# Low weights of the first gate block meet both token tiles at once, and the second tile's norm, quarters and norm row come in another order

## The chip, the cores and the metric

The kernel runs on one core of a Trainium2 chip. A core has five engines with a queue each: TensorE (PE in the profile, with its weight loads as PEld), VectorE (DVE), ScalarE (ACT), GpSimd (POOL) and SyncE (SP, which here only issues DMAs). The metric is the device time of one execution in microseconds; the median of the runs counts.

## The reference

One decoder layer on 256 tokens of width 2048, in float32. The part around the change is the end of the mixing sub-layer and the beginning of the channel mixer:

```python
mix = jnp.concatenate([o_a, o_b], axis=-1) @ w_out[l]
x = x + rmsnorm(mix, post_mix_g[l])
h = rmsnorm(x, pre_ffn_g[l])
u = causal_dwconv(h @ w_up[l], conv_w[l], conv_b[l])
gate, val = jnp.split(u, 2, axis=-1)
y = (jax.nn.gelu(gate, approximate=True) * val) @ w_down[l]
x = x + rmsnorm(y, post_ffn_g[l])
```

`rmsnorm(x, g)` is `x * rsqrt(mean(x*x) + 1e-6) * g` for each token. `w_up` has 2 x 5632 columns; the first 5632 are the gate, the others the value.

## The kernel before

**Products in two parts.** Every float32 operand of a matmul is split into a high part (rounded to the type that TensorE takes) and a low part (what is left), and a product is high x high + high x low + low x high. For weights, ScalarE casts the high part out of a loaded buffer `raw` and VectorE subtracts it to get the low part (`w_split`, lines 112 and 115; `w_high`, lines 95 and 98, where the low part is a function of its own that is called later). There are five `raw` buffers and five slots each for high and low parts, so a load waits for an earlier unit's low part, and a cast waits until TensorE is done with an earlier unit. For activations, `hT` holds for each of 16 chunks of 128 channels (kt) 512 columns: 256 of high parts (128 for each of two token tiles) and 256 of low parts. One matmul of high weights against all 512 columns gives two of the three products; one of low weights against the 256 high columns gives the third. A bank of 512 columns collects them; `conv` (line 908) adds its two halves.

**Around the change.** The output projection's last two column quarters (n = 2 and 3 of four quarters of 512 columns) are computed tile by tile (`out_cols`, line 800). For each, VectorE scales and adds the bank into `mix`, ScalarE squares and sums it into `msq`, and GpSimd multiplies it by the norm's gain `gbc` (`evac_b`, line 747). When a tile has all its sums, `mix_rstd` (line 764) takes VectorE's sum and scaling and GpSimd's power of -1/2, and `residual` (line 769) adds `mix` times that to the tokens `x_sb`, quarter by quarter on VectorE. `turn` (line 773) then transposes a quarter of a tile on TensorE (four transposes into one bank), and its two returned functions write the high parts (ScalarE, line 783) and the low parts (VectorE, line 788) of four chunks of `hT`.

**The first gate block.** The first 256 gate columns have their weights loaded ahead, as four units of four chunks (`gate_unit`, line 828; `lows[0]` to `lows[2]` are the low weights of units 1 to 3). So that TensorE can begin before the second tile is there, `first_gate` (line 924) works tile by tile: `one(t, u)` runs unit u for tile t, eight high products of 256 columns (line 947; that tile's high and low columns) and eight low products (line 943). Units 0 and 1 run their low products for each tile alone, 128 columns; units 2 and 3 run them once, for both tiles, 256 columns, with tile 1. The order on TensorE is: tile 0 units 0 to 2, the sixteen transposes of tile 1, tile 0 unit 3, tile 1 units 0 to 3.

**The norm row.** The second norm's factor for each token is not applied to `hT`; it is made into a row (`rowf`) and multiplied in behind the projection. `x_squares` (line 795) sums each token's squares on ScalarE, four instructions for a tile. `ffn_tables` (line 870) turns them into a factor (VectorE, GpSimd) and a diagonal matrix, and returns `rows`, which transposes the convolution's weights (line 879) and spreads the two diagonals over all partitions by matmul (`row_of`, line 209). `rows` runs in the first value projection (`proj_T4`, line 272) at its first tick, behind the sixteen highs and sixteen lows of units 0 and 1.

**What sets the order.** TensorE's instructions keep the program's order throughout. From line 810 to the end of `first_gate` (line 1074) ScalarE, VectorE and GpSimd keep the order of the text too; instructions from outside this stretch, such as the casts and subtractions of the next projections' weights, may be put between them by a planner that works with estimated times. Elsewhere the planner sets the order of those three engines. `hold.__exit__` (line 859) frees memory that the convolution's table `cst` and the down projection's buffer `extra` take over, so the DMA issues into `cst`, which stand in ScalarE's queue (lines 865 and 866), wait for the last instruction that reads `gbc`.

Of the kernel before, what the change touches and what calls it, by code (L numbers as in the profile page):

```python
# [8 lines left out]
F32 = mybir.dt.float32  # L9
# [8 lines left out]
P = 128  # L18
S = 256
D = 2048  # L20
# [11 lines left out]
def hybrid_layer(ctx: ExitStack, tc: tile.TileContext, x, pre_mix_g, w_in, b_forget, sinks,  # L32
# [27 lines left out]
    def later(n, f):  # L60
        todo.setdefault(now[0] + n, []).append(f)
# [207 lines left out]
            high(*steps[-1])  # L269
            tick()  # L270

    def proj_T4(w, c0, banks):


        parts = {}

        def get(*us):
            for u in us:
                parts[u] = w_split(w_load(w_rows(w, u * 4, 4, c0, 256), 4, 256), still=True)

        def high(kt):
            u, a = divmod(kt, 4)
            for m, b in enumerate(banks):
                pe.matmul(b, parts[u][0][:, a, m * P:(m + 1) * P], hT[:, kt, :],  # L284
                          start=(kt == 0), stop=(kt == KT - 1))

        def low(kt):
            u, a = divmod(kt, 4)
            for m, b in enumerate(banks):
                pe.matmul(b[:, 256:512], parts[u][1][:, a, m * P:(m + 1) * P],  # L290
                          hT[:, kt, 0:256], start=False, stop=False)

        get(0, 1)
        for kt in range(8):
            high(kt)
        for kt in range(8):
            low(kt)
        tick()
        get(2, 3)
        for kt in range(8, 16):  # L300
            low(kt)
        for kt in range(8, 16):
            high(kt)
# [11 lines left out]
    with tc.tile_pool(name="mixp", bufs=1) as mp:  # L315
# [448 lines left out]
        def mix_rstd(t):  # L764
            st = small.tile([P, 1], F32, tag="st", name="st_m")
            dve.tensor_reduce(st, msq[t][:, 0:4 + t], axis=AX.X, op=ALU.add)
            rmix.append(rstd_of(st, D, f"rmix{t}"))

        def residual(t, n):
            xs = x_sb[:, t, n * 512:(n + 1) * 512]  # L770
            dve.scalar_tensor_tensor(xs, mix[t][n], rmix[t], xs, op0=ALU.mult, op1=ALU.add)

        def turn(t, n):

            tb = bank("att")
            for j in range(4):
                c = n * 512 + j * P
                pe.transpose(tb[:, j * P:(j + 1) * P], x_sb[:, t, c:c + P], ident)
            kts = [(n * 4 + j, tb[:, j * P:(j + 1) * P]) for j in range(4)]

            def high():
                for kt, b in kts:
                    act.activation(hT[:, kt, t * P:(t + 1) * P], b, AF.Copy,
                                   scale=gcol[:, 16 + kt:17 + kt])

            def low():
                for kt, b in kts:
                    dve.scalar_tensor_tensor(hT[:, kt, 256 + t * P:256 + (t + 1) * P], b,
                                             gcol[:, 16 + kt:17 + kt],
                                             hT[:, kt, t * P:(t + 1) * P].bitcast(F32),  # L790
                                             op0=ALU.mult, op1=ALU.subtract)

            return high, low
# [51 lines left out]
        lows[0]()  # L845
        for _, low in turns:
            low()
        evac_b(1, 2, out_cols(2, 1, slice(0, 256)), 0)
        lows[1]()
        turns = [turn(0, 2), turn(0, 3)]  # L850
        for high, _ in turns:
            high()
        turns[0][1]()
        evac_b(1, 2, out_cols(2, 1, slice(256, 512)), 1)
        turns[1][1]()
        mix_rstd(1)
        for n in range(4):
            residual(1, n)
        hold.__exit__(None, None, None)

# [1 line left out]
    with tc.tile_pool(name="ffn", bufs=1) as fp:  # L862
# [61 lines left out]
        def first_gate():  # L924

            banks = [bank(), bank()]

            def one(t, u):
                ts = slice(t * P, t * P + P)

                both = u >= 2
                ls = slice(0, 256) if both else ts

                def v(x):
                    return x.rearrange("p (h t c) -> p h t c", h=2, t=2)[:, :, t, :]

                for low in (False, True)[:1 if both and t == 0 else 2]:
                    for kt in range(u * 4, u * 4 + 4):
                        hi, lo = gate[kt]
                        for m, b in enumerate(banks):  # L940
                            ms = slice(m * P, (m + 1) * P)
                            if low:
                                pe.matmul(b[:, 256 + ls.start:256 + ls.stop], lo[:, ms],
                                          hT[:, kt, ls], start=False,
                                          stop=(t == 1 and kt == KT - 1))
                            else:
                                pe.matmul(v(b), hi[:, ms], v(hT[:, kt, :]),
                                          start=(t == 0 and kt == 0), stop=False)

            one(0, 0)  # L950
            one(0, 1)
            one(0, 2)
            for high, low in [turn(1, u) for u in range(4)]:
                high()
                low()
            one(0, 3)
            lows[2]()
            x_squares(0)
            x_squares(1)
            for t in range(2):  # L960
                act.dma_start(x_dram[t * P:(t + 1) * P, :], x_sb[:, t, :])
            rows = ffn_tables()
            for u in range(4):
                one(1, u)
            later(1, rows)
            return banks

        def token_sums(into, y0, y1):

# [94 lines left out]
        for half in range(2):  # L1064
# [4 lines left out]
            for g in range(FHALF // 2):  # L1069
                c0 = (half * (FHALF // 2) + g) * 256  # L1070
                alt = g % 2
                if half == 0 and g == 0:
                    bg = first_gate()
                    order.__exit__(None, None, None)
                    bv = [bank(), bank()]
                    proj_T4(w_up, DFF + c0, bv)
                else:
                    bg = [bank("att"), bank("att")] if alt else [bank(), bank()]
                    proj_T4(w_up, c0, bg)
                gates, ys = [], []  # L1080
# [181 lines left out]
```

## Time and profile before

| | us |
|---|---|
| median of 3 runs | 1063.35 |
| lowest and highest | 1061.34, 1063.37 |
| the profiled execution's own time | 1063.75 |
| its span, first to last instruction | 1062.0 |
| busy in it: TensorE, VectorE, ScalarE, GpSimd | 1047.4, 849.2, 638.4, 227.5 |

The profile is of one execution; all its times count from the start of its span. A row of the chain of waits has a start, a length and a group of instructions; a row of the timeline has a start, a length, engine, line, operation, the tile written and those read, a count, and in brackets how long the engine had been idle and what ended that. Rows of one line's instructions give shortest, median and longest duration in ns. Instructions of an engine overlap a little, so that a group's length over its count is the rate, not the time of one.

### The profile page before, as it was taken

What the parts mean: (1) busy time and instruction counts of PE and PEld (TensorE: products, weight loads), DVE (VectorE), ACT (ScalarE), POOL (GpSimd) and SP (SyncE); (2) the same over time, 40 slices, a digit from 0 to 9 for tenths busy, and PEclk for the clock granted to TensorE, in tenths of its full rate; (3) what the DMA queues carried; (4) which work ended last, traced back from release to release, by engine and by line L of the source; (5) the groups of instructions that cost most, each with busy time, mean ns of one, the idle gap of its engine ahead of it and who ended that gap; (6) DMA issues with size and microseconds to landing.
All of it is one profiled execution on the core that took longest, in us unless ns stands there. A gap on an engine that the chain in (4) does not pass through costs nothing.

```text
span 1062.0 us, 16259 instructions
## 1 busy us (share of the span) xinstructions
PE 1047.4 (99%) x5874; PEld 911.7 (86%) x5874; DVE 849.2 (80%) x1393; ACT 638.4 (60%) x1096; POOL 227.5 (21%) x256
## 2 busy tenths in 40 slices
PE   9999999999999999999999999999999999999995
PEld 7889988888889888888888888888888888888884
DVE  5988888997568887788767989668778787789987
ACT  6767667767547765556555555446556565656551
POOL 3253334441122121212112000012121221200004
PEclk9999999999999999999999999999999999999998
DMA  8645566554863866656665556656566665656562
GB/s 286 211 120 168 164 209 204 177 162 153 301 222 110 293 218 197 192 179 191 194 198 179 198 199 213 220 181 198 168 209 188 192 197 184 196 175 201 196 249 108
DMA packets 154284, 207.08 MB, mean 195 GB/s; under 512 B 6844, under 2 KB 131036, under 8 KB 153180
## 3 DMA queue, kind: packets, MB, share of 16 engines
q1 hardware_dynamic: 153200, 203.37, 59.7%
q10 hardware_dynamic: 1004, 2.68, 0.6%
q8 instruction: 46, 0.75, 0.3%
q14 instruction: 34, 0.28, 0.1%
HBM read 201.68 MB, written 4.21 MB: 194 GB/s over the span
## 4 chain that ended last, share of the span: by engine, by line
PE 75%; DVE 15%; issue 3%; ACT 3%; DMA 2%; POOL 1%; DVEq 0%; SPq 0%; POOLq 0%; ACTq 0%
PE bank_acc L284 15%; PE bank_att L284 14%; PE bank_acc L309 10%; PE bank_acc L290 8%; PE bank_att L290 7%; PE bank_acc L253 7%; DVE wlo L313 6%; PE bank_att L982 4%; PE bank_acc L258 3%; DVE wlo L115 1%; DMA extra<-in_w_down_dram 1%; PE bank_att L475 1%; DVE tb L1026 1%; PE bank_att L511 1%; DVE tb L1023 1%
## 5 line engine op out<-in xcount | busy, mean ns | idle before, releaser
L115 DVE TENSOR_TENSOR wlo<-raw,whi 128x1024 fp32r<-128x1024 f32 (+3 forms) x271 | 329.9, 1228 | 123.6 <-ACT whi L112 116.2
L112 ACT CAST whi<-raw 128x1024 fp32r<-128x1024 f32 (+3 forms) x270 | 273.1, 1029 | 128.2 <-issue 86.0
L914 POOL TENSOR_TENSOR room<-room,rowf 128x256 f32<-128x256 f32 x88 | 100.3, 1160 | 393.9 <-DVE room L913 392.0
L284 PE MATMUL bank_acc<-hT,whi 128*128 128x512 f32 x736 | 173.3, 390 | 0.0
L284 PEld LDWEIGHTS bank_acc<-hT,whi 128*128 128x128 f32 x736 | 136.4, 188 | 27.4
L982 PE MATMUL bank_att<-whi,G 128*128 128x512 f32 x488 | 156.1, 389 | 0.0
L284 PE MATMUL bank_att<-hT,whi 128*128 128x512 f32 x640 | 150.6, 390 | 0.0
L284 PEld LDWEIGHTS bank_att<-hT,whi 128*128 128x128 f32 x640 | 118.7, 188 | 23.9
L982 PEld LDWEIGHTS bank_att<-whi,G 128*128 128x128 f32 x488 | 91.6, 188 | 18.8
L982 PE MATMUL bank_att<-wlo,G 128*128 128x512 f32 x244 | 95.2, 390 | 0.1
L290 PEld LDWEIGHTS bank_acc<-hT,wlo 128*128 128x128 f32 x736 | 89.3, 188 | 2.0
L290 PE MATMUL bank_acc<-hT,wlo 128*128 128x256 f32 x736 | 89.8, 279 | 0.0
L916 ACT ACTIVATE room<-room,cw 128x256 f32<-128x256 f32 x88 | 53.0, 602 | 60.5 <-POOL room L914 60.5
L253 PE MATMUL bank_acc<-hT,whi 128*128 128x512 f32 x352 | 88.0, 395 | 0.0
L309 PE MATMUL bank_acc<-whi,oT 128*128 128x512 f32 (+1 forms) x272 | 81.7, 379 | 0.0
L290 PEld LDWEIGHTS bank_att<-hT,wlo 128*128 128x128 f32 x640 | 77.6, 188 | 1.7
L290 PE MATMUL bank_att<-hT,wlo 128*128 128x256 f32 x640 | 77.9, 279 | 0.0
L918 DVE SCALAR_TENSOR_TENSOR room<-room,cw 128x256 f32<-128x256 f32 x88 | 62.4, 709 | 17.6 <-ACT room L916 17.3
L253 PEld LDWEIGHTS bank_acc<-hT,whi 128*128 128x128 f32 x352 | 63.3, 188 | 11.5
L313 DVE TENSOR_TENSOR wlo<-raw,whi 128x1024 fp32r<-128x1024 f32 (+1 forms) x56 | 61.3, 1118 | 11.9 <-ACT whi L312 11.9
L312 ACT CAST whi<-tb 128x1024 fp32r<-128x1024 f32 x42 | 44.0, 1049 | 44.2 <-PE bank_att L982 19.4
L312 ACT CAST whi<-raw 128x1024 fp32r<-128x1024 f32 (+1 forms) x56 | 52.3, 958 | 26.6 <-PE bank_att L982 17.1
(251 smaller groups left out, 1594.4 us busy)
## 6 DMA issues: line engine op xcount, KB each, us to landing
raw<-in_w_up_dram SPq DMA_DIRECT2D x176, 512.0 KB, 4.3
raw<-in_w_down_dram SPq DMA_DIRECT2D x58, 512.0 KB, 5.1
raw<-in_w_in_dram SPq DMA_DIRECT2D x51, 512.0 KB, 4.6
raw<-in_w_out_dram SPq DMA_DIRECT2D x32, 512.0 KB, 3.9
extra<-in_w_down_dram SPq DMA_DIRECT2D x20, 512.0 KB, 4.5
raw<-in_w_in_dram SPq DMA_DIRECT2D x16, 384.0 KB, 3.5
tb<-in_w_down_dram SPq DMA_DIRECT2D x10, 512.0 KB, 3.5
cb<-c_dram SPq DMA_DIRECT2D x8, 256.0 KB, 3.9
```

The lines of the kernel that those rows point to most:

```text
L112: i1 = act.copy(hi[:, cs], raw[:, cs])
L115: i2 = dve.tensor_tensor(lo[:, cs], raw[:, cs], hi[:, cs].bitcast(F32), op=ALU.subtract)
L253: pe.matmul(b, parts[u][0][:, a, m * P:(m + 1) * P], hT[:, kt, :], start=(kt == 0), stop=(kt == KT - 1))
L284: pe.matmul(b, parts[u][0][:, a, m * P:(m + 1) * P], hT[:, kt, :], start=(kt == 0), stop=(kt == KT - 1))
L290: pe.matmul(b[:, 256:512], parts[u][1][:, a, m * P:(m + 1) * P], hT[:, kt, 0:256], start=False, stop=False)
L309: pe.matmul(b, a, r[:, cols], start=(first and i == 0), stop=(last and i == 2))
L312: act.copy(hi, src)
L313: dve.tensor_tensor(lo, src, hi.bitcast(F32), op=ALU.subtract)
L914: pool.tensor_tensor(u[:, 2:258], u[:, 2:258], rowf, op=ALU.mult)
L916: act.activation(y, u[:, 2:258], AF.Identity, bias=cw[:, 3, ch:ch + 1], scale=cw[:, 2, ch:ch + 1])
L918: dve.scalar_tensor_tensor(y, u[:, 1:257], cw[:, 1, ch:ch + 1], y, op0=ALU.mult, op1=ALU.add)
L982: pe.matmul(b[:, to] if to else b, a, r[:, cols], start=(first and i == 0), stop=(last and i == 2))
```

## The change

The first half of the diff concerns the second tile's norm. The last column quarter's two halves of tile 1 are no longer evacuated by `evac_b`. For the first half, the squares and the gain multiply are separate (`square_b`) and ScalarE's square stands between the high parts of tile 0's quarters 2 and 3. The other quarters' sums are taken beforehand (`mix_others`), and the second half's squares are summed and added to them by one fused instruction on VectorE; GpSimd's power follows at once, and that half's gain multiply comes behind it. The first tile's squares for the norm row (`x_squares(0)`) move ahead of the second tile's residuals, of which quarter 2's moves behind quarter 0's low parts.

The second half concerns TensorE's order. All high products of tile 0 run first, then the transposes of tile 1's quarters 0, 1 and 3, then units 0 to 3 of tile 1, each with its high products and its low products for both tiles at once; quarter 2's transposes stand behind unit 0. The low weights of unit 2 (`lows[1]`) are made later, behind quarter 1's low parts. `rows` now runs in the value projection behind its first eight high products instead of at the first tick.

```diff
-    def proj_T4(w, c0, banks):
+    def proj_T4(w, c0, banks, between=None):
...
         for kt in range(8):
+            if between and kt == 4:
+                between()
             high(kt)
...
+        def mix_others():
+            st = small.tile([P, 1], F32, tag="st", name="st_m")
+            dve.tensor_reduce(st, msq[1][:, 0:4], axis=AX.X, op=ALU.add)
+            v = small.tile([P, 1], F32, tag="rv", name="rv")
+            dve.tensor_scalar(v, st, 1.0 / D, EPS, op0=ALU.mult, op1=ALU.add)
+            return v
+
+        def square_b(t, n, h):
+            m = mix[t][n][:, h * 256:h * 256 + 256]
+            act.activation(junk[:, 0:256], m, AF.Square, accum_out=msq[t][:, n:n + 1])
+            pool.tensor_tensor(m, m, gbc[:, n * 512 + h * 256:n * 512 + h * 256 + 256],
+                               op=ALU.mult)
...
-            def low():
-                for kt, b in kts:
+            def low(part=slice(0, 4)):
+                for kt, b in kts[part]:
...
-        evac_b(1, 2, out_cols(2, 1, slice(0, 256)), 0)
-        lows[1]()
+        b12 = out_cols(2, 1, slice(0, 256))
+        dve.scalar_tensor_tensor(mix[1][2][:, 0:256], b12[:, 0:256], rstd_b[1], mix[1][2][:, 0:256],
+                                 op0=ALU.mult, op1=ALU.add)
         turns = [turn(0, 2), turn(0, 3)]
-        for high, _ in turns:
-            high()
+        turns[0][0]()
+        square_b(1, 2, 0)
+        turns[1][0]()
         turns[0][1]()
-        evac_b(1, 2, out_cols(2, 1, slice(256, 512)), 1)
-        turns[1][1]()
-        mix_rstd(1)
-        for n in range(4):
+        v = mix_others()
+        turns[1][1](slice(0, 2))
+        b12 = out_cols(2, 1, slice(256, 512))
+        m12 = mix[1][2][:, 256:512]
+        dve.scalar_tensor_tensor(m12, b12[:, 256:512], rstd_b[1], m12, op0=ALU.mult, op1=ALU.add)
+        ms = small.tile([P, 1], F32, tag="rv", name="ms")
+        dve.tensor_tensor_reduce(mix[0][0][:, 0:256], m12, m12, 1.0 / D, v, ALU.mult, ALU.add, ms)
+        r12 = small.tile([P, 1], F32, tag="rmix1", bufs=2, name="rmix1")
+        pool.tensor_tensor(r12, ms, mhalf, op=ALU.pow)
+        rmix.append(r12)
+        pool.tensor_tensor(m12, m12, gbc[:, 1280:1536], op=ALU.mult)
+        turns[1][1](slice(2, 4))
+        x_squares(0)
+        for n in (0, 1, 3):
             residual(1, n)
         hold.__exit__(None, None, None)
...
-            one(0, 0)
-            one(0, 1)
-            one(0, 2)
-            for high, low in [turn(1, u) for u in range(4)]:
-                high()
-                low()
-            one(0, 3)
+            def highs(t, u):
+                for kt in range(u * 4, u * 4 + 4):
+                    for m, b in enumerate(banks):
+                        pe.matmul(v(b, t), gate[kt][0][:, m * P:(m + 1) * P], v(hT[:, kt, :], t),
+                                  start=(t == 0 and kt == 0), stop=False)
+
+            def both_low(u):
+                for kt in range(u * 4, u * 4 + 4):
+                    for m, b in enumerate(banks):
+                        pe.matmul(b[:, 256:512], gate[kt][1][:, m * P:(m + 1) * P],
+                                  hT[:, kt, 0:256], start=False, stop=(kt == KT - 1))
+
+            for u in range(4):
+                highs(0, u)
+            t0, t1, t3 = (turn(1, n) for n in (0, 1, 3))
+            t0[0]()
+            t0[1]()
+            residual(1, 2)
+            highs(1, 0)
+            both_low(0)
+            t2 = turn(1, 2)
+            t1[0]()
+            t1[1]()
+            lows[1]()
+            t3[0]()
+            t2[0]()
+            t2[1]()
+            t3[1]()
             lows[2]()
-            x_squares(0)
             x_squares(1)
             for t in range(2):
                 act.dma_start(x_dram[t * P:(t + 1) * P, :], x_sb[:, t, :])
             rows = ffn_tables()
-            for u in range(4):
-                one(1, u)
-            later(1, rows)
-            return banks
+            for u in range(1, 4):
+                highs(1, u)
+                both_low(u)
+            return banks, rows
...
-                    bg = first_gate()
+                    bg, rows = first_gate()
                     order.__exit__(None, None, None)
                     bv = [bank(), bank()]
-                    proj_T4(w_up, DFF + c0, bv)
+                    proj_T4(w_up, DFF + c0, bv, rows)
```

More of the change, by code (lines that the diff above doesn't have):

```diff
@@ L926, in first_gate @@
             banks = [bank(), bank()]
[L928 to L948, printed above, removed]
@@ L950, in first_gate, with v @@
-            one(0, 0)
-            one(0, 1)
-            one(0, 2)
-            for high, low in [turn(1, u) for u in range(4)]:
-                high()
-                low()
-            one(0, 3)
+            def v(x, t):
+                return x.rearrange("p (h t c) -> p h t c", h=2, t=2)[:, :, t, :]
+            def highs(t, u):
[3 more added lines that the diff above has]
+                                  start=(t == 0 and kt == 0), stop=False)
```

## The prediction

> **What bounds the kernel now.** I read the page first, for the span and for the chain that ended last.
>
> ```profile
> span 1062.0 us, 16259 instructions
> PE 75%; DVE 15%; issue 3%; ACT 3%; DMA 2%; POOL 1%; DVEq 0%; SPq 0%; POOLq 0%; ACTq 0%
> ```
>
> TensorE carries three quarters of the chain, so a change pays only where TensorE is in it. The change lies between the end of the output projection and the first value projection. The busy times of that stretch, and then its chain of waits (start, length, group), settle who is in it there:
>
> ```profile
> 331.50:346.40 14.90, 14.90 (x131) 14.90 (x130) 13.36 (x35) 10.48 (x33) 1.44 (x6) 1.00 0.48 156
> 331.67 0.96 PE bank_acc L947 x8
> 332.63 0.84 PE bank_acc L943 x8
> 333.47 0.99 PE bank_acc L947 x8
> 334.46 0.84 PE bank_acc L943 x8
> 335.31 1.00 PE bank_acc L947 x8
> 336.31 1.75 PE bank_att L778 x16
> 338.06 1.92 PE bank_acc L947 x16
> 339.97 0.84 PE bank_acc L943 x8
> 340.81 0.99 PE bank_acc L947 x8
> 341.81 0.84 PE bank_acc L943 x8
> 342.65 1.00 PE bank_acc L947 x8
> 343.64 0.94 PE bank_acc L943 x8
> 344.58 0.95 PE bank_acc L947 x8
> 345.54 0.94 PE bank_acc L943 x8
> 346.48 3.65 PE bank_acc L284 x16
> ```
>
> TensorE is busy for all 14.90 us, at a granted clock of 1.00, and the chain runs through its matmuls without a break. So VectorE (13.36) and ScalarE (10.48) are covered here, and only two things can move the time: TensorE work that goes, and a wait on TensorE that is new. Each L943 group of 0.84 is eight low products of 128 columns; the two of 0.94 are eight of 256.
>
> **Low products.** Four narrow groups and two wide ones, 4 x 0.84 + 2 x 0.94 = 5.24, become four wide ones, 4 x 0.94 = 3.76: 1.48 less. The narrow matmul has half the columns and costs 0.105 us against 0.117, so something other than columns sets its price. The Trainium skill, "TensorE: Matmul & The Clock Gate", section "Back-to-back issue gap", prices an isolated warm matmul at about N/2.4 ns + 2.5; by that two of 128 columns cost what one of 256 does and this edit would save next to nothing. The 0.84 row speaks against it. The same page, "LDWEIGHTS (loading the stationary operand)", gives a load about P/1.2 ns, an estimate of 107 ns for 128 columns, and with that floor the trace agrees.
>
> **High products.** The same 64 remain. Behind narrow lows eight took 0.99 or 1.00, elsewhere 0.95 or 0.96: 0.96 + 0.99 + 1.00 + 1.92 + 0.99 + 1.00 + 0.95 = 7.81. I take 8 x 0.96 = 7.68 afterwards, 0.13 less. TensorE's work falls by 1.61 in all; the 16 transposes and the norm row stay.
>
> **The second tile's norm.** These rows are of VectorE, GpSimd, ScalarE (its own DMA issues are ACTq) and, for the fused reduction, the attention's form of it:
>
> ```profile
> 331.96 0.47 DVE L751 SCALAR_TENSOR_TENSOR mix_sb<-bank_acc,rg,mix_sb 128x256 f32<-128x256 f32 x1
> 334.38 2.74 DVE L771 SCALAR_TENSOR_TENSOR x_sb<-mix_sb,rmix,x_sb 128x512 f32<-128x512 f32 x4 [0.67 <-POOL rmix L183]
> 333.05 0.74 POOL L753 TENSOR_TENSOR mix_sb<-mix_sb,gbc_mix 128x256 f32<-128x256 f32 x1 [2.06 <-ACT junk L752]
> 333.80 0.55 POOL L183 TENSOR_TENSOR rmix<-rv,mhalf 128x1 f32<-128x1 f32 x1
> 333.83 1.68 ACTq L865 DMA_DIRECT2D cst<-in_conv_w_dram  x3
> 335.53 0.38 ACTq L866 DMA_DIRECT2D cst<-in_conv_b_dram  x1
> L481 DVE CUSTOM_DVE_ANT_0 p<-bank_att,p,nsnk x32: 319/410/485, 46.3 to 129.0; 128x256 f32<-128x256 f32 x16, 128x128 f32<-128x128 f32 x16
> ```
>
> Before, the last quarter's evacuation starts at 331.96 and the first residual at 334.38. Afterwards VectorE waits for TensorE's last output product (331.67), evacuates in 0.47 to about 332.2, squares and sums in one instruction, GpSimd takes the power (0.55), and the residuals start near 333.35, 1.0 earlier. The fused instruction reads SBUF only, which no row here shows; the attention's reads PSUM at 0.32 to 0.49. I take 0.41 as the nearest, plus some 0.1 for its sum; free would move the residuals 0.5 forward, twice the price 0.5 back. That the earlier start is worth nothing follows below: the transposes come at 335.5 and have 1.4 us of cover. Were that gone, every microsecond of it would show on TensorE.
>
> The gain multiply of that quarter moves behind the power: 333.3 to 334.1 on GpSimd. Four DMA issues stand in ScalarE's queue behind it, since they fill memory that it still reads: before they start at 333.83, right at its end, and hold the queue to 335.91. Now they hold it from 334.1 to 336.2. The first tile's squares come ahead of them, in time when ScalarE waited, and cost nothing.
>
> **The new wait.** The second tile's quarter passes transposes, ScalarE high part, VectorE low part:
>
> ```profile
> 337.96 4.23 DVE L788 SCALAR_TENSOR_TENSOR hT<-bank_att,gcol,hT 128x128 fp32r<-128x128 f32 x16 [0.84 <-ACT hT L783]
> L788 DVE SCALAR_TENSOR_TENSOR hT<-bank_att,gcol,hT x32: 340/342/353, 326.7 to 341.9; 128x128 fp32r<-128x128 f32 x32
> 336.78 4.25 ACT L783 ACTIVATE hT<-bank_att,gcol 128x128 fp32r<-128x128 f32 x16 [3.81 <-PE bank_att L778]
> 342.11 1.22 DVE L98 TENSOR_TENSOR wlo<-raw,whi 128x1024 fp32r<-128x1024 f32 x1
> ```
>
> From the first transpose (336.31) to ScalarE is 0.47, from there to VectorE's first low 1.18. VectorE's lows follow every 0.26 and last 0.34. Before, sixteen transposes and the eight highs of tile 0's last unit stood between a quarter's transposes and its first use. Afterwards tile 0's highs all run first: 331.67 + 4 x 0.96 = 335.51. Twelve transposes at 0.109 end at 336.82, and then TensorE wants quarter 0 at once. ScalarE starts on it at 336.2 (335.98 without the DMA issues), VectorE at 337.4, the fourth low ends at 338.5, and two more matmuls end at 338.7. Undisturbed this group would end at 336.82 + 0.96 = 337.78. TensorE waits about 1.0; 0.7 if the DMA issues are out of the way, 1.4 if the fused instruction costs double and delays them. Everything behind on TensorE's queue is delayed with it.
>
> Behind that wait it gets tight but holds. Lows of unit 0 to 339.66, four transposes to 340.10, highs of unit 1 to 341.06: VectorE has done residual 2 (0.69) and the fourth low of quarter 1 by 340.2, needed at 340.8. Unit 1's lows end at 342.00. The low weights of unit 2 now stand here on VectorE, 340.1 to 341.3; quarter 2's fourth low ends at 342.4, needed at 342.7. Quarter 3's lows end at 343.4 and unit 3's low weights at 344.6, needed at 344.9. The gate ends at 345.8 against 346.48. Either slack of 0.3 is lost if one weight subtraction of 1.22 is put between: 0.9 each.
>
> **The row placed earlier.** It is now asked for after eight highs of the value projection, 345.8 + 8 x 0.228 = 347.6, and, behind the 0.31 of the small transposes, at 347.9. Its last input is tile 1's squares. The rows: the chain's, then ScalarE's (the casts of 340.8 to 350.3 as a group, then single ones), VectorE's, SyncE's, and the loads by the page.
>
> ```profile
> 352.00 0.31 PE bank_att L879 x4
> L112 ACT CAST whi<-raw 128x1024 fp32r<-128x1024 f32 x4 | 4.4, 1099 | 0.0
> 344.79 0.63 ACT L797 ACTIVATE junk<-x_sb 128x512 bf16<-128x512 f32 x1
> 345.54 0.63 ACT L797 ACTIVATE junk<-x_sb 128x512 bf16<-128x512 f32 x1
> 346.17 1.04 ACT L112 CAST whi<-raw 128x1024 fp32r<-128x1024 f32 x1
> 347.12 0.62 ACT L797 ACTIVATE junk<-x_sb 128x512 bf16<-128x512 f32 x1
> 350.08 0.19 ACT L797 ACTIVATION_READ_ACCUMULATOR junk<-x_sb 128x1 f32 x1
> 351.52 0.29 DVE L203 TENSOR_SCALAR diag<-ident,rffn 128x128 f32<-128x128 f32 x1 [0.66 <-POOL rffn L183]
> 330.46 0.37 SPq L69 DMA_DIRECT2D raw<-in_w_up_dram  x1
> raw<-in_w_up_dram SPq DMA_DIRECT2D x176, 512.0 KB, 4.3
> ```
>
> A square takes a slot of 0.75, a weight cast between squares 0.95, and from the last square's sum (350.27) to the diagonal (351.81) it is 1.54. ScalarE is through with quarter 2 at 341.2. Four squares and no cast give a diagonal at 345.8; two casts, the share that the planner mixed in before (four among eight squares), give 347.7; three 348.6. So no wait, by 0.2; with three casts 0.7. The row's later users (the convolution) get it about 4 us earlier, which TensorE doesn't feel: its chain has no break there.
>
> **Loads.** The low weights of unit 2 free a load buffer, whose refill in SyncE's queue was issued at 330.46. It moves to 341.3 and lands 4.3 later, at 345.6; the value projection wants its low part at about 352.5, so some 5 us remain for cast and subtraction. No cost.
>
> **The sum.** -1.61 + 1.0 = -0.6 on the profiled execution, whose own time is 1063.75 around a span of 1062.0: 1063.15. The median of the three runs is 1063.35, 0.40 below it, so 1062.8. Runs that lie 2 us apart make 0.2% (2.1 us, so 1061.2 to 1065.5) about what can be told from no change, and both terms and their bounds (-0.9 to -0.2) are inside.
>
> **Rivals.**
>
> *Slower: the row waits for weights.* Place: ScalarE's queue ahead of tile 1's last square. If the planner puts the cast of the next block's first unit there, that cast needs a buffer freed at 344.6 and landing at 348.9; then 0.95 for the cast, 0.75 for the square and 1.54 give a diagonal at 352.1, and TensorE waits 4.2: +3.6, 1066.9. It decides from the fourth cast on. For it: four casts precede the last square before, among eight squares. Against: only four squares are left there. 0.12. The trace has a granted clock of 1.00 here and no such wait, so it can't show what one does to the clock. The Trainium skill, "TensorE: Matmul & The Clock Gate", Part 1, halves the clock after an idle window of some 3.4 us: by it this rival costs up to an estimated 1.7 more; no run here shows it.
>
> *Faster: the order downstream changes.* Outside the hand-written stretch the planner sets ScalarE's and VectorE's order, and the down projection's chain goes through it:
>
> ```profile
> 574.15 2.81 issue
> ```
>
> If the shifted times make it drop such a hole, -2.8 comes on top of -0.6: 1060.0. For it: VectorE's 15% of the chain. Against: nothing in the edit touches those lines, and the opposite shift, to 1065.6, is as possible. 0.18 for the first, 0.06 for the second.
>
> *The wait eats the gain.* One weight subtraction in one of the slacks of 0.3 above: +0.9, 1063.7. 0.15, no change that can be measured.
>
> *The lows save nothing.* If cost went by moving columns, the four narrow groups would be worth 4 x 0.47, the sum would lose its 1.48, and 1064.3 would result (the rule of the page above). The 0.84 rows refute it: 0.02.
>
> **How the numbers follow.** My forecast has 0.47, 1062.8, with 1061.5 to 1064.0 as its own range. No change by over 0.2% holds 0.47 + 0.15 + 0.02 = 0.64; faster 0.18; slower 0.12 + 0.06 = 0.18. The range 1060.7 to 1065.4 leaves out the slow rivals and the far end of the fast one.
>
> **What would show it.** Right: the chain has L943's successor in groups of 0.94 only, no narrow lows; a hole of about 1 us on TensorE before tile 1's first highs, ended by VectorE's low part; the gate's end 0.4 to 0.9 earlier; the row's transposes some 2 us behind it. Wrong: a hole at the row's matmuls ended by the diagonal; a second one before unit 2's or 3's products; or a time outside 1061.2 to 1065.5 with the gate's end as forecast, which would put the cause downstream.

## The result, and the profile after

The changed kernel takes 1065.83 us (median of 9 runs, 1063.99 to 1066.83) where the kernel before takes 1063.37 beside it (9 runs, 1061.34 to 1063.86 but for one of 3733.8, which the ratio leaves out): a ratio of 1.0027 with a 95% interval of 1.0019 to 1.0035. It is slower by about 2.5 us, outside the predicted range and in the other direction. The profiled execution is the fastest of the nine (1063.99, span 1062.3), so it need not show all that the median pays.

The page gives the span and, at its fourth part, the engines' shares of the chain that ended last:

```profile
span 1062.3 us, 16229 instructions
PE 79%; DVE 11%; issue 3%; ACT 3%; DMA 2%; POOL 1%; SPq 0%; DVEq 0%; POOLq 0%; ACTq 0%
```

TensorE's share rose by four points, but a share of the whole says nothing of one stage. The chain of waits of the changed kernel from the end of the output projection to the second gate block (start, length, group) does; lines 961 and 967 are the gate's high and low products, 209 the row, 284 the highs of the value projection and of the next gate block:

```profile
331.03 3.84 PE bank_acc L961 x32
...
336.52 0.36 DVE hT L803
...
336.92 1.34 PE bank_acc L961 x8
338.27 0.94 PE bank_acc L967 x8
...
345.50 1.47 POOL rffn L183
...
346.99 0.04 DVE diag L203
...
348.62 0.56 POOL rffn L183
...
349.20 0.30 DVE diag L203
...
349.55 0.49 PE bank_att L209 x2
350.03 1.84 PE bank_acc L284 x8
...
359.26 2.95 PE bank_att L284 x13
```

The chain now leaves TensorE twice. Before, the second gate block began at

```profile
358.30 3.63 PE bank_att L284 x16
```

so that the stage from the first gate highs (331.67) to there took 26.63; now it takes 359.26 - 331.03 = 28.23, 1.60 more. The span grew by 0.3 only, because the stage began 0.64 earlier (331.03 against 331.67) and what follows it took 703.0 instead of 703.7. The earlier start is not the edit's: TensorE was already 0.64 ahead at the transposes of 323.54 (324.18 before), ahead of the edited lines, and the start scatters, from 330.91 to 331.59 in the four profiled executions of the changed kernel. The shorter rest is not scatter: it is 702.9 to 703.2 in the ten profiles of the changed kernel and those made from it, and 703.7 and 703.9 in the two of the kernel before. So some 0.7 is gained behind the stage, where the forecast has only its faster rival, with 2.8; where it comes from stays open.

TensorE's timeline shows the same two holes; the bracket is the time that it had been idle, and what ended that:

```profile
336.92 1.34 PE L961 MATMUL bank_acc<-hT,whi 128*128 128x256 f32 x8 [0.74 <-DVE hT L803]
347.42 0.42 PE L209 MATMUL bank_att<-diag,ones 128*128 128x128 f32 x2
349.55 0.49 PE L209 MATMUL bank_att<-diag,ones 128*128 128x128 f32 x2 [1.71 <-DVE diag L203]
```

The first hole was forecast, the second was not: two of the row's four matmuls wait 1.71 us for the second tile's diagonal. The account closes. Forecast work -1.61; first hole 0.74, and the eight highs behind it 1.34 instead of 0.95, as the later groups take: 0.39; the row's hole 1.71, and its two matmuls 0.49 instead of half of 0.48: 0.25. That is 1.48 of the 1.60; unit 2's highs for tile 1 (1.07 to 1.08 against 0.95 in the chains of `subs_behind` and `rows_back`) are the rest. The expectations below count a hole from start to start beyond the usual rate; so counted the two are 0.91 and 1.87.

Here is why the second diagonal is late. VectorE's timeline of the changed kernel:

```profile
344.07 0.15 DVE L900 TENSOR_REDUCE st_x<-sqm 128x1 f32<-128x4 f32 x1
344.14 1.21 DVE L115 TENSOR_TENSOR wlo<-raw,whi 128x1024 fp32r<-128x1024 f32 x1
345.27 0.15 DVE L181 TENSOR_SCALAR rv<-st_x 128x1 f32<-128x1 f32 x1
345.33 1.22 DVE L115 TENSOR_TENSOR wlo<-raw,whi 128x1024 fp32r<-128x1024 f32 x1
346.99 0.29 DVE L203 TENSOR_SCALAR diag<-ident,rffn 128x128 f32<-128x128 f32 x1 [0.44 <-POOL rffn L183]
347.20 0.15 DVE L900 TENSOR_REDUCE st_x<-sqm 128x1 f32<-128x4 f32 x1
347.26 1.22 DVE L115 TENSOR_TENSOR wlo<-raw,whi 128x1024 fp32r<-128x1024 f32 x1
348.39 0.15 DVE L181 TENSOR_SCALAR rv<-st_x 128x1 f32<-128x1 f32 x1
```

Between one tile's reduction (L900), scaling (L181) and diagonal (L203) stand the value projection's weight subtractions (L115), three of 1.2 us, and tile 1's reduction stands behind tile 0's diagonal. ScalarE had been done long before; the only cast among tile 1's squares and their last row are

```profile
341.31 1.06 ACT L112 CAST whi<-raw 128x1024 fp32r<-128x1024 f32 x1
...
344.32 0.19 ACT L812 ACTIVATION_READ_ACCUMULATOR junk<-x_sb 128x1 f32 x1
```

The last square's sum is there at 344.51; the second diagonal ends at 349.49, 4.98 later, where the forecast had 1.54.

### The profile page after: what moved, and what is told of

It reads as the page before. It is cut to its first block, busy times and chain, and to the rows that moved or that the text cites. A ratio compares the mean times of both kernels' runs of the same rounds, so it can differ in the third digit from the quotient of the medians.

```text
span 1062.3 us, 16229 instructions
## 1 busy us (share of the span) xinstructions
PE 1045.0 (98%) x5858; PEld 908.8 (86%) x5858; DVE 848.3 (80%) x1395; ACT 638.2 (60%) x1094; POOL 230.2 (22%) x256
## 4 chain that ended last, share of the span: by engine, by line
PE 79%; DVE 11%; issue 3%; ACT 3%; DMA 2%; POOL 1%; SPq 0%; DVEq 0%; POOLq 0%; ACTq 0%
PE bank_acc L284 15%; PE bank_att L284 14%; PE bank_acc L311 10%; PE bank_att L1010 9%; PE bank_acc L290 8%; PE bank_att L290 7%; PE bank_acc L253 7%; DVE wlo L315 4%; PE bank_acc L258 3%; PE bank_acc L1010 2%; DVE wlo L115 2%; PE bank_att L477 1%; PE bank_att L513 1%; ACT whi L112 1%; DMA x_in<-in_x_dram 1%
## 5 line engine op out<-in xcount | busy, mean ns | idle before, releaser
L115 DVE TENSOR_TENSOR wlo<-raw,whi 128x1024 fp32r<-128x1024 f32 (+3 forms) x271 | 329.9, 1228 | 124.4 <-ACT whi L112 117.0
L290 PEld LDWEIGHTS bank_acc<-hT,wlo 128*128 128x128 f32 x736 | 89.3, 188 | 2.0
L290 PE MATMUL bank_acc<-hT,wlo 128*128 128x256 f32 x736 | 89.6, 280 | 0.0
L290 PEld LDWEIGHTS bank_att<-hT,wlo 128*128 128x128 f32 x640 | 77.6, 188 | 1.7
L290 PE MATMUL bank_att<-hT,wlo 128*128 128x256 f32 x640 | 77.9, 280 | 0.0
```

The costliest lines, as they stand in the source:

```text
L115: i2 = dve.tensor_tensor(lo[:, cs], raw[:, cs], hi[:, cs].bitcast(F32), op=ALU.subtract)
```

## The experiments

The theory of the loss: VectorE's order makes the row's hole, so it goes with the row's new place or with the subtractions. Its rivals: the joined low products and what the planner makes of them downstream; the clock behind a hole; the DMA issues in ScalarE's queue. Each expectation names its theories A and B anew. The number of a run is the median of its kernel; the kernel before ran beside each (1062.8 to 1062.9).

**The kernel before, unchanged** (`control`).

> The kernel before once more, unchanged, for its spans and granted clocks run by run. Theory A (the waits at TensorE's queue are the whole price, and the rest of the difference is how long the core stays at the low clock at the start): its clocks scatter as the changed kernel's do, 0.995 to 0.997, and its time is 1063 within 0.7. Theory B (a TensorE wait of 1.9 us costs clock besides itself): its clocks are higher run for run than the 0.995 that most runs of the changed kernel show, 0.996 to 0.997.

Measured: 1063.33 against 1062.76, ratio 1.0004 (0.9995 to 1.0013). So differences of half a microsecond tell nothing here. Its eleven mean clocks are 0.996 or 0.997 and never 0.995, as theory B had it.

**The row back at the first tick** (`rows_back`), the rest of the change kept.

```diff
-            return banks, rows
+            later(1, rows)
+            return banks
...
-                    proj_T4(w_up, DFF + c0, bv, rows)
+                    proj_T4(w_up, DFF + c0, bv)
```

> The changed kernel with the norm row put back to the first tick of the value projection. Theory A: the wait of 1.9 us at the row goes, since its diagonal comes near 349.5 and is now asked for behind sixteen lows, after 350.5; the other wait of 0.9 stays. Time 1.9 below the changed kernel, 1063.9, and within 0.1% of before. Theory B (the price lies in the clock or in the order downstream, not in this wait): less than half of it comes back, 1064.9 or more.

Measured: 1062.94 against 1062.76, ratio 1.0006 (0.9997 to 1.0014); the loss is gone, and with it the row's hole. The time is 1.0 lower than theory A's 1063.9, and no mean clock is 0.995. The gain isn't there either, and its chain says where it went:

```profile
351.18 0.52 DVE cw L907
...
352.00 1.23 DVE wlo L115
...
353.27 0.74 PE bank_acc L290 x4
```

The subtraction of the value projection's unit 3 stood in VectorE's queue behind the copies that wait for the row (L907 and L908), and the low products (L290) waited 0.72 for it (0.88 counted from start to start). The stage takes 358.11 - 330.91 = 27.20 by the same chain, 0.57 over before.

**The row's new place alone**, in the kernel before (`row_alone`).

```diff
+            if between and kt == 4:
+                between()
...
-            later(1, rows)
-            return banks
+            return banks, rows
```

> The kernel before with the row alone asked for earlier, behind eight highs of the value projection. Theory A: TensorE comes to the diagonals at 346.5 + 1.8 + 0.3 = 348.6, the second is ready at 351.8 to 352.9, so a wait of 3.2 to 4.3 and a time of 1066.6 to 1067.7. Theory B: with a wait twice as long as the changed kernel's, the clock falls too, and it is over 1068. If the row's place costs nothing: 1063.4.

Measured: 1067.53 against 1062.76, ratio 1.0039 (1.0026 to 1.0052). The row waits longer than in the changed kernel, since the squares end later, and the next two answers (timeline, then busy times by window, whose number behind the five engines is the granted clock) show a second price:

```profile
351.90 0.79 PE L209 MATMUL bank_att<-diag,ones 128*128 128x128 f32 x2 [2.64 <-DVE diag L203]
```

```profile
351.40:354.90 3.50, 3.00 (x8) 2.52 (x9) 1.06 (x3) 0.99 (x3) 0.77 (x2) 0.51 1.04 382
354.90:358.00 3.10, 3.10 (x26) 2.97 (x26) 2.25 (x5) 3.07 (x4) 0.91 (x1) 1.00 1.00 409
```

For 3.4 us, from half a microsecond before the hole's end, the clock is at half, and 8 matmuls run in that window where the next 3.1 us hold 26. The time is in theory A's range, but not for theory A's reason alone: the wait was shorter than its 3.2 to 4.3, and the clock, theory B's, paid the rest.

**The joined lows alone**, in the kernel before (`lows_only`).

```diff
-                both = u >= 2
+                both = u >= 0
```

> The kernel before with the merged low products alone: all four units run their lows once for both tiles, with tile 1; norm, order of transposes and row as before. TensorE's work falls by 1.6, but it reaches the second tile's transposes 1.7 earlier, before the residuals that they read (334.4 to 337.1, one every 0.67), and waits about 1.2 there. Theory A: 0.4 faster, 1063.0, and narrow groups of 0.84 gone from the chain. If a matmul's price went by its columns the work would not fall, and it would be 1.2 slower.

Measured: 1066.28 against 1062.76, ratio 1.0032 (1.0020 to 1.0044). Slower, and not by the columns: the low groups take 0.94 each in its chain, as forecast. Theory A's 1063.0 is missed all the same. TensorE waits at tile 1's transposes, as expected (0.64 in front of them, and the sixteen take 2.64 instead of 1.91), and at a place that nobody expected, in the second gate block. VectorE's timeline there:

```profile
360.99 0.87 DVE L918 SCALAR_TENSOR_TENSOR room<-room,cw 128x256 f32<-128x256 f32 x2
361.79 0.87 DVE L920 SCALAR_TENSOR_TENSOR room<-room,cw 128x256 f32<-128x256 f32 x2
362.58 0.75 DVE L1090 TENSOR_TENSOR room<-room 128x256 f32<-128x256 f32 x2
...
363.65 1.21 DVE L115 TENSOR_TENSOR wlo<-raw,whi 128x1024 fp32r<-128x1024 f32 x1
```

The planner put the convolution ahead of a weight subtraction, and low products waited 1.52 and 0.81 for it and the next (idle times). The edit names none of these lines. So the downstream order does move, as the rival of the prediction had it, and here in the bad direction. In the changed kernel itself no such hole is there. The six runs scatter from 1063.63 to 1068.05 with mean clocks of 0.994 to 0.998, so a part of this median may be the clock's; the profiled one has no halved stretch there.

**The changed kernel again** (`after_look_a`, `after_look_b`, unaltered, one profiled execution each), to see whether the first profile was typical.

> The changed kernel once more, unchanged, for one more look at where its clock is granted. The row alone had a stretch of 3.4 us at half clock behind its wait of 2.8. Theory B: an execution of the changed kernel at 0.995 and over 1065.5 shows such a stretch at 348 to 354, behind the wait of 1.9; one at 0.997 and under 1065 does not. Theory A: no such stretch, and the clock differs by when it first rises (4 to 10 us) alone.

> The same look again: with the first one and the profile there are three executions of the changed kernel, and by theory B about two in three have the stretch at half clock.

Measured: 1065.53 and 1064.93 against 1062.93. The row's hole is 1.87 again in both; the clock stays at 1.00 behind it. But the first hole is 1.81 and 1.73 instead of 0.91. The chain of `after_look_a` (ACTq is ScalarE issuing DMAs):

```profile
334.24 0.32 ACTq L892
...
334.59 1.35 ACTq L892
...
336.81 0.36 ACT hT L798
...
338.39 1.35 PE bank_acc L961 x8
```

The second of the four issues into the convolution's table took 1.35 us (0.30 in the profile above), and ScalarE came to quarter 0 that much later. In the kernel before the issues scatter too (three of them took 1.68 in its profile and 1.96 in the control's, and the second of them 0.69 and 0.98), but there ScalarE had until 336.78.

**The subtractions behind the diagonals** (`subs_behind`): the changed kernel, with the value units' subtractions held behind both tiles' chains on VectorE.

```diff
-            if pin:
+            if pin or after:
                 tc.keep_in_program_order(i2)
...
-                parts[u] = w_split(w_load(w_rows(w, u * 4, 4, c0, 256), 4, 256), still=True)
+                parts[u] = w_split(w_load(w_rows(w, u * 4, 4, c0, 256), 4, 256), still=True,
+                                   after=between is not None)
```

> The changed kernel with the value units' weight subtractions kept behind both tiles' diagonals on VectorE; the two tiles' chains still run one behind the other. Theory A (the three subtractions of 1.2 us between the chains' steps made the row late): the second diagonal is there at 346.0 to 346.5, the row doesn't wait, and the time falls by the row's 1.9 to about 1063.6. Rival B (it is the two chains one behind the other, each with GpSimd's power in it): the second diagonal comes at 348.5 or later and a wait of 1 us or more stays at the row.

Measured: 1062.46 against 1062.91, ratio 0.9998 (0.9989 to 1.0007). The row's hole is gone. VectorE's timeline, then the chain:

```profile
345.43 0.15 DVE L901 TENSOR_REDUCE st_x<-sqm 128x1 f32<-128x4 f32 x1
345.61 0.15 DVE L181 TENSOR_SCALAR rv<-st_x 128x1 f32<-128x1 f32 x1
346.43 0.28 DVE L203 TENSOR_SCALAR diag<-ident,rffn 128x128 f32<-128x128 f32 x1 [0.66 <-POOL rffn L183]
346.63 2.35 DVE L115 TENSOR_TENSOR wlo<-raw,whi 128x1024 fp32r<-128x1024 f32 x2
```

```profile
331.18 3.84 PE bank_acc L962 x32
...
339.80 0.95 PE bank_acc L962 x8
...
341.69 1.07 PE bank_acc L962 x8
...
347.73 0.48 PE bank_att L209 x4
...
357.45 3.63 PE bank_att L285 x16
```

The two chains still run one behind the other, and the second diagonal is there at 346.71, 2.05 behind the last square's sum (344.66 here): theory A had 346.0 to 346.5, rival B 348.5 or later. The stage takes 26.27, 0.36 less than before: -1.61 + 0.75 + 0.39 + 0.12 = -0.35, with the first hole's 0.75, the 0.39 behind it and 1.07 against 0.95. That is the size of what the change was good for without the row's hole.

**Tile 0's chain early** (`table0_early`): the reduction, factor and diagonal of tile 0 stand behind quarter 0's high parts; the subtractions stay where the planner puts them.

```diff
+        def table_of(t):
+            st2 = small.tile([P, 1], F32, tag="st", name="st_x")
+            dve.tensor_reduce(st2, sq2[t], axis=AX.X, op=ALU.add)
+            dffn.append(diag_of(rstd_of(st2, D, f"rffn{t}")))
...
             t0[0]()
+            table_of(0)
             t0[1]()
```

> The changed kernel with tile 0's reduction, factor and diagonal early, behind the first highs; the subtractions still stand between the steps of tile 1's chain, two of them ahead of its diagonal and one or both beside GpSimd's power. Theory A (each subtraction ahead of the second diagonal costs its 1.2): one subtraction less is ahead of it, and tile 0's chain is out of the way, so the diagonal comes about 2 earlier, at 347.3 to 347.8, and 0 to 0.3 of the row's wait of 1.87 is left. Rival B (the wait is set by something behind VectorE's order, such as GpSimd or the squares on ScalarE): 1 us or more of it stays. Time by A about 1063.8.

Measured: 1063.19 against 1062.91, ratio 1.0004 (0.9995 to 1.0013). Of the row's hole 0.24 is left (its four matmuls take 0.72 where 0.48 is usual). The absolute times in the expectation missed, since this execution's first hole was 1.50 and shifted everything; the size of what is left is as theory A has it. Two subtractions still stand between tile 1's steps (345.87 and 347.06), the second beside GpSimd's power: with tile 0's chain out of the way, two cost 0.24, where three and tile 0's chain cost 1.87.

**Both edits together** (`chain_first`).

> The changed kernel, its row where the change puts it, but the norm's small instructions ahead of the weight subtractions on VectorE: tile 0's are done behind the first quarter's high parts, tile 1's come before the four subtractions of the first value projection, which are held behind them. Theory A and B alike (the diagonal is late because subtractions of 1.2 stand between its steps): the diagonal follows the last square (344.5) by about 1.3, at 345.8, is asked for at 347.3, the wait of 1.9 is gone, the wait of 0.9 at the first quarter stays, the clock doesn't fall, and the time is 1063.0 to 1063.6. If the diagonal were late for another reason (squares, GpSimd), at least 1 us of the wait stays and the time is 1064.8 or more.

Measured: 1063.31 against 1062.93, ratio 1.0004 (0.9995 to 1.0013). No hole at the row; the profiled execution is 1061.92, but three of eleven lie at 1064.0 to 1064.7 with a mean clock of 0.995 (a fourth, at 1064.4, has 0.996). What cost these the clock no profile shows.

**A cover for the first wait** (`chain_cover`): the same, with tile 0's last highs between the transposes of quarters 1 and 3, and the four DMA issues in SyncE's queue.

```diff
-            act.dma_start(cst[:, k, :], conv_w[k].rearrange("(a p) -> a p", p=P))
-        act.dma_start(cst[:, 3, :], conv_b[0].rearrange("(a p) -> a p", p=P))
+            sp.dma_start(cst[:, k, :], conv_w[k].rearrange("(a p) -> a p", p=P))
+        sp.dma_start(cst[:, 3, :], conv_b[0].rearrange("(a p) -> a p", p=P))
...
-            for u in range(4):
+            for u in range(3):
                 highs(0, u)
-            t0, t1, t3 = (turn(1, n) for n in (0, 1, 3))
+            t0, t1 = (turn(1, n) for n in (0, 1))
+            highs(0, 3)
+            t3 = turn(1, 3)
```

> As the last, and the first wait covered too: tile 0's last eight highs stand between the transposes of quarters 1 and 3, and the four DMA issues into the convolution's table go through SyncE's queue instead of ScalarE's. If the wait of 0.9 is for quarter 0's way through ScalarE and VectorE with nothing to cover it, 0.3 of it stays and the time is 0.6 under the last, about 1062.5; if it is a price of something else, nothing changes.

Measured: 1062.69 against 1062.93, ratio 0.9996 (0.9987 to 1.0005). The one hole of 0.91 became two, of 0.27 and 0.25, but little was gained by it: the eight highs behind still take 1.34, and the transposes, now asked for earlier, wait for residuals (the first is done at 334.81 and quarter 0's start at 334.86; the second at 335.47 and quarter 1's at 335.52). The stage takes 26.15, and 26.26 in `chain_first`. So the 0.6 between the two medians, which the expectation had, is not shown to be the cover's: none of these eleven runs has a mean clock of 0.995, and the two intervals overlap. It is no measurable gain over the kernel before either, nor is `subs_behind`; the two are the only ones whose medians lie under it.

**The DMA issues alone moved to SyncE's queue** (`sp_issue`), in the changed kernel, and **the changed kernel once more** (`after_look_c`).

> The changed kernel with one edit: the four DMA issues into the convolution's table stand in SyncE's queue instead of ScalarE's. Theory A (the first wait is 0.9 in one execution and 1.7 to 1.8 in others because these issues hold ScalarE for 2 to 3 us): ScalarE starts on quarter 0 as soon as its transposes are there, the wait in front of tile 1's first highs is 0.7 to 0.8 in the profile whatever the execution, the row's wait of 1.87 stays, and the time falls to 0.5 to 1.0 under the changed kernel's of the same call, about 1064.8. Rival B (the issues aren't what holds quarter 0; the fused reduction and the residuals are): the wait stays at 0.9 or more and the time within 0.4 of the changed kernel's.

> The changed kernel once more, unaltered, on the chip of this call, so that the three edits can be compared with it. Theory A (first wait 0.9 to 1.8 by the execution, row's wait 1.87 in each): time 2.0 to 2.8 above the kernel before; the row's wait is 1.87 again and the first wait lies between 0.9 and 1.85. Rival B (the waits read from the first profile are chance): a row's wait under 1.5 or above 2.3.

Measured: 1065.22 and 1066.13 against 1062.91, ratios 1.0022 (1.0013 to 1.0032) and 1.0025 (1.0014 to 1.0036). The intervals overlap, and both profiles show the same two holes as the first one (0.91 and 1.87), so whether the issues matter to the median is not told apart by these runs: the first wait is rival B's, the 0.9 between the medians theory A's. They showed something else. Windows behind the row's hole, first of the first profile of the changed kernel, then of `after_look_c`:

```profile
350.00:353.50 3.50, 3.50 (x25) 3.17 (x24) 2.22 (x4) 0.74 (x1) 1.33 (x2) 1.00 1.04 354
```

```profile
350.00:353.50 3.50, 3.50 (x11) 2.78 (x12) 2.22 (x4) 0.39 (x1) 1.15 (x2) 0.57 1.02 358
```

And the chain of `after_look_c`:

```profile
331.35 3.84 PE bank_acc L961 x32
...
350.35 3.18 PE bank_acc L284 x8
...
361.13 0.91 PE bank_att L284 x4
```

Eight highs took 3.18 instead of 1.84. The clock fell to half for 3.4 us behind a hole that is as long as in the first profile (1.72 against 1.71), and the stage took 361.13 - 331.35 = 29.78, 1.55 more than there. `sp_issue` shows the same: 0.52 in that window. So the clock's rival, which `after_look_a` and `after_look_b` had not shown, is real, but not in every execution. The mean clock of each run suggests how often: of 18 executions of the changed kernel 12 have 0.995, with a mean time of 1066.2, 5 have 0.997, with 1064.6, and one has 0.996. The five profiles with this hole fit: the two with a halved stretch have 0.995 (one of them `sp_issue`'s), the three without it 0.997. The 1.6 between the two means is about half of 3.4. What else is in the mean clock can be counted: in every profile here the clock also falls to half at the end, when TensorE has run out of work, for 6.2 to 9.1 us, which alone makes a mean of 0.9957 to 0.9971; 3.4 us more at half take another 0.0016. So 0.995 points to a halved stretch, 0.996 decides nothing, and the mean doesn't say where the stretch lay. Of the 28 runs of the kernel before in the last comparison one has 0.995.

The Trainium skill, "TensorE: Matmul & The Clock Gate", Part 1, says that the clock falls to half after an idle window of about 3.4 us, that the window runs free of the program, and that the same time brings the clock back. The length of the halved stretch agrees (3.4 us in three profiles). The idle time does not need to fill a window: 1.71 us was enough in some executions. That it was not in others fits a window that runs free, and so does where the stretch begins: 0.64 and 0.71 us behind the hole's end in `after_look_c` and `sp_issue`, half a microsecond before it in `row_alone`. No run here shows the window itself.

## Why the prediction was wrong

**What held.** The low products went to four groups of 0.94, and the columns rival is refuted. The fused instruction took 0.49 plus 0.08 for its sum, where 0.51 was taken; tile 1's residuals began 1.0 earlier against the stage's start, as forecast. (The first of them took 1.22 where the others take 0.74. It began at 332.75, within GpSimd's gain multiply of 332.68 to 333.41, which the change put there and the forecast gave no price; the cover that it counted on hid the 0.5.) The new wait for quarter 0 is there, ended by VectorE, and cost 0.74 + 0.39 in the profiled execution, where 1.0 was forecast; the slacks of 0.3 behind it held but for the 0.12 at unit 2's highs, and the gate's end came 0.40 earlier against the stage's start, where 0.7 was forecast. `subs_behind` has what these terms make together: -0.36, where -0.6 was forecast.

**The step that failed: "The row placed earlier".** One cast stood among the four squares where the forecast took two (the other came ahead of quarter 2's high parts), and the last square's sum came 1.0 earlier against the stage's start than it had said: that part erred on the safe side. The failed term is the 1.54 from the last square's sum to the diagonal. It was read from tile 1 in the kernel before, where no subtraction stood between the steps. The changed kernel took 4.98, because three weight subtractions and tile 0's whole chain came first. The sign follows from it: no wait by 0.2 became a hole of 1.71, which with the 0.25 of its matmuls is 1.96 of the 2.2 between the stage's +1.60 and the forecast's -0.6. `rows_back` and `subs_behind` take the hole away from two sides, `table0_early` all but 0.24 of it from a third. The profile of before had the warning: tile 0's own chain, in VectorE's timeline, a few rows above the one that was used.

```profile
345.54 0.16 DVE L873 TENSOR_REDUCE st_x<-sqm 128x1 f32<-128x4 f32 x1
345.62 1.23 DVE L115 TENSOR_TENSOR wlo<-raw,whi 128x1024 fp32r<-128x1024 f32 x1
346.76 0.15 DVE L181 TENSOR_SCALAR rv<-st_x 128x1 f32<-128x1 f32 x1
347.24 1.23 DVE L115 TENSOR_TENSOR wlo<-raw,whi 128x1024 fp32r<-128x1024 f32 x1 [0.33 <-ACT whi L112]
348.39 0.28 DVE L203 TENSOR_SCALAR diag<-ident,rffn 128x128 f32<-128x128 f32 x1
```

There the same four steps took 3.1 us, with two subtractions between them. With that for tile 1 the forecast diagonal would have come about 1.6 after 347.7, and the row would have waited some 1.4.

**The slower rival had the wrong queue.** It put the row's wait down to a fourth cast in ScalarE's queue, 4.2 us long. The place, the hole at the row ended by the diagonal, was right; the queue was VectorE's. Its sentence on the clock was right in kind, but it went by the idle window of some 3.4 us that the Trainium skill states, and the forecast's own case got no such price; 1.71 was enough.

**Two sizes were taken as fixed that scatter.** The DMA issues in ScalarE's queue were taken at 2.08 together; a longer second issue made the first hole 1.7 to 1.8 in two of four profiled executions of the changed kernel. And the halved clock, which the forecast had only in a rival, adds about 1.6 in the executions that have it, most of them by their mean clocks. The stage's +1.6, the clock's 1.6 and the 0.7 gained behind the stage make +2.5 with a short first hole and about 0.9 more with a long one; the medians are 2.5 and, in the last comparison, 3.2 above the kernel before. How often the clock falls rests on the mean clocks, not on a profile of each run.

**"Loads ... No cost"** held in the changed kernel, but narrowly: with the row back in its place the moved unit's subtraction came late, by 0.72.

## What to carry over

When a chain of short steps is asked for earlier, count what an order-setting planner may put between every two of its steps, and take the price from every instance in the trace, the worst first. A hole on TensorE of under 2 us can cost as much again by the clock, and not in every execution, so several profiles are needed before one is called typical. An issue time or a wait that is covered in one order of work may scatter unseen; when the cover is taken away, its scatter counts.

## What had not been expected of the hardware

- The clock fell to half for 3.4 us behind idle times of 1.71 and 1.72 (two of five profiled executions) and 2.64, and not in the other three of 1.71.
- A power of one column on GpSimd took 0.55, but 1.46 where it began inside a weight subtraction on VectorE: it began at 345.50, the subtraction ran from 345.33 to 346.55, and the power ended 0.4 behind it. The Trainium skill, "SBUF — State Buffer", section "SBUF: two separate sides", has GpSimd and a VectorE instruction with two inputs from SBUF lock each other out of a shared port for a whole instruction; the trace agrees, and shows it the other way round too: the residual that began within a gain multiply took 1.22 instead of 0.74. A subtraction that began at 347.24, within a power of 346.99 to 347.55 in the kernel before, took its usual 1.23 all the same.
- The second of the four DMA issues in ScalarE's queue took 0.30 in two profiles of the changed kernel, 1.29 and 1.35 in the other two, and 1.04 in `table0_early`; the others took 0.37 to 0.56. What stretched it stays open: SyncE issued a DMA at the same time in the stretched ones and in the others.
- The eight highs behind the first hole took 1.34 to 1.35 in the chain instead of 0.95 in every kernel that has the hole. The first of them took 0.39 instead of 0.28, and the low parts that they read, one for two of them, come from VectorE every 0.26; how much of it is the stop and how much the low parts was not separated.
